# Splitting values that land by transposing transfers without priority, and leaving more work between the transfers out and back

## The chip, the cores and the metric

The kernel runs on one core of a Trainium2 chip. The metric is the device time of one execution in microseconds (us). The kernel before was run three times: 1028.9, 1032.0 and 1032.71 us, a median of 1032.0 us. TensorE (PE) multiplies matrices into PSUM banks; VectorE (DVE) and ScalarE (ACT) do elementwise work; GpSimd (POOL) does a few powers; SyncE (SP) issues nearly all transfers between the chip's main memory and the on-chip memory, and ACT issues a few.

## The reference

A sequence of 512 tokens of width 1024, with 16 learned meta tokens put in front, goes through two layers, and a final norm drops the meta tokens. Layer 0 is gated linear attention with 4 heads (keys of 256, values of 512); layer 1 is differential softmax attention with 8 heads (values of 256). Both have a wide input projection, a SiLU gate and an output projection:

```python
h = concat([meta, x])                          # 528 tokens
for i in range(2):
    hn = rmsnorm(h, g_norm[i])
    y = gla_branch(hn, ...) if i == 0 else diff_branch(hn, ...)
    h = h + y
return rmsnorm(h[:, 16:], g_final)

# gla_branch: q, k, v, z, g = split(hn @ w_in); decay = cumulative log-sigmoid of g
#   o = causal(q k^T with decay) v, per head;  y = silu(z) * head_rms(o) * gnorm;  y @ w_out
# diff_branch: q, k, v, z = split(hn @ w_in); p0, p1 = softmax(q k^T + bias) of two halves
#   o = (p0 - lam * p1) v, per head;  y = silu(z) * head_rms(o) * gnorm;  y @ w_out
```

All data are 32-bit floats. Every operand of a precise matmul is split into a high and a low part, and three products of the parts are summed.

## The kernel before

**Layout.** Activations stand with features on the 128 partitions and the 528 tokens along the row. A projection therefore gives q, k, v and z in this layout, too. The attention needs the values with tokens on the partitions, so v must be transposed, and then split into high and low parts for the matmuls that read it (the pair `s.v`, and `s.vm` for the 16 tokens left over of a multiple of 128).

**How v is turned.** In the heads 1 to 3 of layer 0, in two halves each, and once in each of the heads 1 to 6 of layer 1, this goes by way of main memory (`turn_by_dma`, L521): 12 times in all. It has four steps:

- `leave` (L530): ACT copies one of two blocks of v into 16-bit planes (L532) and issues the transfer out, to the buffer `vd` (L533). It runs once for each of the two blocks.
- `turn` (L538): SP issues transposing transfers back into the same place (L541; tile `keep` in layer 0, one each; `planes` in layer 1, two each) and one more, of the ends, into the single buffer `lands` (L543).
- `done` (L821 in layer 0, L1457 in layer 1): the landed values are split, ACT writing the high part (L262) and DVE the low part (L263), each about a microsecond of 128 x 1024 elements; and the ends are split by `split3`, two operations on ACT (L355, L356) and one on DVE (L360).
- The attention of that head reads the result: in layer 0 from `gla_blocks` on (L1129, first at L1141), in layer 1 in the step `values` of `diff_steps` (L1578).

Head 0 of layer 0, and the first and last heads of layer 1, turn v with TensorE instead and are not touched.

**Fill.** The `Weaver` W (L74) holds a queue of generators that emit projection matmuls a few at a time and state a cost in microseconds for each. The attention code calls `W.fill(us)` between its own steps so that TensorE always has something to do. `W.follow((a, f), (b, g))` calls f when a us of such fill have been emitted, and g when b us more have. `W.land()` (L1239, L1703), before a head's attention, calls whatever is left at once. A projection is emitted by `Unit` (L384): seven products of 12 matmuls each, with the first product of the next unit drawn ahead of the last two of its own.

**Order.** TensorE's instructions run in the order in which the program emits them (L212). For ACT, DVE and SP the framework makes an order: it goes through the program with its own reckoning of durations and gives each engine, when free, the operation of the best rank among those that it reckons ready. The rank is the place in the program; `@urgent` (L251) improves it by 100 places. The order is fixed at build time, so on the chip an engine waits at an operation whose input is late, with all that stands behind it.

**Other lines that the text names.** Weight loads are L271 and L278 (tile `raw`); weights are split at L262 and L263 (`wh`/`wl`, `a11h`/`a11l`, `a12`, `a22`); sums of weight blocks are L318 (`sum`, `raw`). `u` (L400) is a copy of a product on ACT, `t` L425 and L427 are the sums that finish a projection on DVE. L899 adds the output projection into `hT`, and TensorE's next product into the same bank (L891) waits for it. `on` (L1583, L1586) normalizes a block of attention rows in layer 1, and TensorE transposes it at L1592. `aT` and `am` are the split attention weights, `k` the split keys.

Of the kernel before, what the change touches and what calls it, by code (L numbers as in the profile page):

```python
# [150 lines left out]
class Weights:  # L151
# [44 lines left out]
    def done(self, p):  # L196
        self.room[p.kind] += 1
        self.pump()
# [8 lines left out]
def trunk(ctx, tc, x, meta, g_norm, gla_w_in, gla_w_gate_up, gla_b_gate, gla_gnorm, gla_w_out,  # L207
# [21 lines left out]
    def T(p, shape, dt, tag, **kw):  # L229
        uid[0] += 1  # L230
        return p.tile(shape, dt, tag=tag, name=f"{tag}_{uid[0]}", **kw)
# [27 lines left out]
    def split(hi, lo, src, scale=None):  # L259

        if scale is None:
            act.activation(hi, src, AF.Copy)  # L262
            dve.tensor_tensor(lo, src, hi.bitcast(F32), op=ALU.subtract)  # L263
        else:
            act.activation(hi, src, AF.Copy, scale=scale)
            dve.scalar_tensor_tensor(lo, src, scale, hi.bitcast(F32), op0=ALU.mult, op1=ALU.subtract)
# [27 lines left out]
    W = Weaver()  # L294
# [14 lines left out]
    def want_unit(w, c0):  # L309
        def single(tag, b):  # L310
            def fn(raw):
                t = [T(wp, [P, 512], F32R, tag + part, bufs=1) for part in "hl"]
                split(*t, raw[:, b, :])
                return t
            return Part(tag, fn)

        def add(o, a, b):
            dve.tensor_tensor(o, a, b, op=ALU.add)  # L318

        def sums(raw):  # L320
            t = T(wp, [P, 2, 512], F32, "sum", bufs=1)
            add(t[:, 1, :], raw[:, 2, :], raw[:, 3, :])
            add(t[:, 0, :], t[:, 1, :], raw[:, 0, :])
            add(raw[:, 2, :], raw[:, 2, :], raw[:, 0, :])
            return t

        def outer(raw):
            add(raw[:, 1, :], raw[:, 1, :], su.t[:, 0, :])
            ws.room["sum"] += 1
            return block_pair(raw[:, 1:3, :])  # L330

        a11, a12, a22 = single("a11", 0), single("a12", 1), single("a22", 3)
        su = Part("sum", sums)
        s21 = Part("pair", lambda raw: block_pair(su.t))
        s43 = Part("pair", outer)
        ws.want((w, c0), [a11, su, s21, a12, s43, a22])
        return a11, a12, a22, s21, s43
# [12 lines left out]
    def split3(dst, src, lo, scale=None):  # L350


        kw = {} if scale is None else {"scale": scale}
        hi = dst[:32].bitcast(F32)
        act.activation(dst[:32], src, AF.Copy, **kw)  # L355
        act.activation(dst[96 - lo:128 - lo], src, AF.Copy, **kw)  # L356
        if scale is None:
            dve.tensor_tensor(dst[lo:lo + 32], src, hi, op=ALU.subtract)
        else:
            dve.scalar_tensor_tensor(dst[lo:lo + 32], src, scale, hi, op0=ALU.mult, op1=ALU.subtract)  # L360
# [152 lines left out]
    def tmp():  # L513
        return T(tp, [P, L], F32, "t")


    def words(t):

        return t.bitcast(U16)

    def turn_by_dma(planes, groups, ends, done):  # L521

        n = planes.shape[2]
        vd = T(dp, [2, P, 2, n], U16, "vd", bufs=3)
        rows = vd.rearrange("m p h c -> (m p h) c")
        raw = planes.rearrange("p m c -> p (m c)")[:, :2 * NR].rearrange("p (b c) -> p b c", c=2 * P)
        left, lands = [0, 1], []

        @urgent
        def leave(m, src):  # L530
            pl = words(planes[:, m, :]).rearrange("p (h c) -> p h c", h=2)
            act.activation(pl, words(src).rearrange("p (c h) -> p h c", h=2), AF.Copy)  # L532
            act.dma_start(vd[m], pl)  # L533
            left.remove(m)
            if not left:
                W.follow((6.0, turn), (9.0, lambda: done(raw, lands[0][:32, 0, :])))

        def turn():  # L538
            for blocks, c0 in groups:
                o = words(raw[:, blocks, :])  # L540
                sp.dma_start(o, rows[:, c0:c0 + P * o.shape[1]], transpose=True)  # L541
            lands.append(T(mp, [P, 1, 2 * P], F32, "lands"))
            sp.dma_start(words(lands[0]), rows[:, ends:ends + P], transpose=True)  # L543

        return leave
# [237 lines left out]
    def to_tokens(vt, blocks, short_cols):  # L783


        pt, pm = ps_tile(), ps_tile()[:32, :P]
        for b, (t0, n) in enumerate(blocks[1:]):
            pe.transpose(pt[:, b * P:(b + 1) * P], vt[:, t0:t0 + n], ident)
        pe.transpose(pm, short_cols, ident)
        return pt, pm  # L790

    def plain_unit(u, evac):

        (a11, a22), (a12, a21) = [ws.use(h) for h in u]
        for i, (wa, wb) in enumerate(((a11, a12), (a21, a22))):
            banks = pb_pair()
            for j, (w, xs) in enumerate(((wa, (X["b11"], b12)), (wb, (X["b21"], X["b22"])))):
                for n, (k, p, q) in enumerate(PASSES):
                    for bank, x in zip(banks, xs):
                        pe.matmul(bank[:, :HT], w[p][:, k * P:(k + 1) * P], x[q][:, k, :],  # L800
                                  start=j == n == 0, stop=j == 1 and n == len(PASSES) - 1)
                    if n % 3 == 2:
                        yield 0.66
            evac(i, banks)
        for h in u:
            ws.done(h)

    def q_gla_v(hd, s):
        us = [want_unit(g_w_in, 2048 + 512 * hd + c) for c in (0, 256)] if hd else v_first

        def turned_back(m, vt):
            def post():
                pt, pm = to_tokens(vt, BLK, vt[:, :32])
                cs = slice(m * P, (m + 1) * P)
                split(s.v[0][:, :, cs], s.v[1][:, :, cs], pt.rearrange("p (b c) -> p b c", b=4))
                split3(s.vm[:, cs], pm, 32, short[:, NM:NM + 1])
            W.defer(2.4, post)

        def turner(h):
            @urgent  # L820
            def done(pt, pm):  # L821
                cs = slice(256 * h, 256 * h + 256)
                split(s.v[0][:, :, cs], s.v[1][:, :, cs], pt)
                split3(s.vm[:, cs], pm, 32, short[:, NM:NM + 1])
            return turn_by_dma(b_all[:, 2 * h:2 * h + 2, :], [(slice(0, 4), NM)], 0, done)

        gens = []
        for h, u in enumerate(us):
            vts = []

            def dst(h=h, vts=vts):
                if h == 0:
                    s.vm = T(gp, [M3, 512], F32R, "vm0")
                    s.v = [T(gp, [P, 4, 512], F32R, f"v{i}") for i in range(2)]
                vts.extend([tmp(), tmp()])
                return vts

            if hd:
                gens.append(W.add(Unit(u, X, 1.0, dst, lambda i, vts=vts, leave=turner(h): leave(i, vts[i]))))
            else:  # L840
                def evac(i, banks, h=h, vts=vts, dst=dst):
                    if i == 0:
                        dst()
                    for n, bank in enumerate(banks):
                        act.activation(vts[i][:, n * HT:(n + 1) * HT], bank[:, :HT], AF.Copy)
                    turned_back(2 * h + i, vts[i])

                gens.append(W.add(plain_unit(u, evac)))
        return gens[0]
# [593 lines left out]
    def turned_back2(s, m, vt, first=False):  # L1443
        if not first:

            urgent(dve.tensor_copy)(vt[:, HT:HT + 8], vt[:, 2 * HT:2 * HT + 8])

        @urgent
        def post():
            end = L if first else 272  # L1450
            pt, pm = to_tokens(vt, RBLK if first else HBLK, vt[:, end - 32:end])
            cs = slice(m * P, (m + 1) * P)
            split3(s.vm[:, cs], pm, 32, short[:, NM + 1:NM + 2])
            split(s.v[0][:, :, cs], s.v[1][:, :, cs], pt.rearrange("p (b c) -> p b c", b=4))

        @urgent
        def done(pt, pm):  # L1457
            split3(s.vm, pm, 32, short[:, NM + 1:NM + 2])
            split(s.v[0], s.v[1], pt)

        if first or s is heads[-1]:
            W.defer(2.2 if first else 1.4, post)
        else:
            if m:
                s.leave = turn_by_dma(T(ep, [P, 2, 536], F32, "planes", bufs=1),
                                      [(slice(3, 1, -1), 0), (slice(1, None, -1), 272)], 240, done)
            s.leave(m, vt[:, :536])
# [346 lines left out]
```

## Time and profile before

| what | value |
|---|---|
| median of three runs | 1032.0 us |
| the profiled execution | 1031.73 us |
| its span, first to last instruction | 1029.9 us |
| mean granted TensorE clock | 0.983 |
| busy, share of the span: PE, DVE, ACT, POOL | 95%, 76%, 60%, 5% |
| transfers out to `vd` on ACT, of 264 or 268 KB | 24 |
| transposing transfers on SP (L541 and L543) | 18 and 12 |

A row of the profile names the engine, the line of the kernel, the operation, the tile written and the tiles read, and their sizes. Waits are put down to what came last by the profile. The granted clock is the share of full speed that TensorE was given in a stretch. Idle time of an engine costs nothing by itself; it counts where TensorE waits for that engine.

### The profile page before, as it was taken

Reading aid. Unit: us, or ns where it says so; the run is one execution under the profiler, and the core shown is the slowest. Engines: PE = TensorE matmul, PEld = TensorE weight load, DVE = VectorE, ACT = ScalarE, POOL = GpSimd, SP = SyncE. Lnnn points to the kernel's source line nnn. Section 1 sums busy time; section 2 is a strip of 40 time slices with the busy share of each in tenths; the row PEclk is TensorE's granted clock in tenths of the full one; section 3 lists DMA queues with packets and bytes.
Section 4 is the critical chain, followed back from the end, with each engine's and each line's share of the span. In section 5 each row is a group of like instructions: output and inputs, shape, how many; then the busy total and the mean of one; then the engine's idle time right before and its main releaser. Section 6 shows DMA issues by size and latency. Waiting matters only on the chain. (4 is left out here: it accounts for less than half of the span.)

```text
span 1029.9 us, 18079 instructions
## 1 busy us (share of the span) xinstructions
PE 983.0 (95%) x7023; PEld 922.1 (90%) x7023; DVE 778.1 (76%) x1562; ACT 613.3 (60%) x1292; POOL 48.2 (5%) x68
## 2 busy tenths in 40 slices
PE   8999999899999998999999998998989999999997
PEld 7999999899989997999999797897978989978996
DVE  7888886687767886556996985877856868667785
ACT  6775756366626666536766674475654666645574
POOL 1000000000000100000001010000000000100001
PEclk8999999999999999999999999999999999999999
DMA  7222226331443354222323424234242333523212
GB/s 194 74 70 65 78 84 169 77 94 42 140 119 83 82 114 113 74 83 82 93 83 101 121 74 126 65 103 118 82 140 80 91 94 83 139 82 93 82 63 81
DMA packets 156296, 98.63 MB, mean 96 GB/s; under 512 B 38429, under 2 KB 142141, under 8 KB 156208
## 3 DMA queue, kind: packets, MB, share of 16 engines
q1 hardware_dynamic: 152752, 90.92, 32.8%
q10 hardware_dynamic: 3456, 6.54, 1.8%
q8 instruction: 55, 0.90, 0.4%
q14 instruction: 33, 0.27, 0.1%
HBM read 83.64 MB, written 8.66 MB: 90 GB/s over the span
## 5 line engine op out<-in xcount | busy, mean ns | idle before, releaser
L263 DVE TENSOR_TENSOR wl<-raw,wh 128x1024 fp32r<-128x1024 f32 x99 | 120.9, 1223 | 29.1 <-ACT wh L262 20.4
L262 ACT ACTIVATE wh<-raw 128x1024 fp32r<-128x1024 f32 x99 | 103.9, 1052 | 44.7 <-PE by L891 18.5
L379 PE MATMUL bv<-x,wh 128*128 128x264 f32 (+1 forms) x656 | 97.5, 287 | 3.2 <-DVE t L427 3.2
L379 PE MATMUL bx<-x,wh 128*128 128x264 f32 (+1 forms) x640 | 96.4, 288 | 4.2 <-ACT u L400 4.1
L379 PEld LDWEIGHTS bx<-x,wh 128*128 128x128 f32 x640 | 85.4, 190 | 5.8 <-ACT u L400 5.0
L379 PEld LDWEIGHTS bv<-x,wh 128*128 128x128 f32 x656 | 86.6, 189 | 3.9 <-DVE t L427 3.4
L369 PE MATMUL bx<-x,wh 128*128 128x512 f32 (+1 forms) x256 | 64.5, 395 | 2.6 <-ACT ps L1582 1.6
L263 DVE TENSOR_TENSOR wl<-sum,wh 128x1024 fp32r<-128x1024 f32 x41 | 50.1, 1222 | 21.0 <-ACT wh L262 19.6
L400 ACT ACTIVATE u<-bx 128x264 f32<-128x264 f32 (+1 forms) x120 | 45.4, 379 | 31.8 <-PE bx L379 28.5
L262 ACT ACTIVATE wh<-sum 128x1024 fp32r<-128x1024 f32 x41 | 43.2, 1054 | 25.3 <-PE by L891 8.6
L1549 ACT ACTIVATE p<-p,st 128x528 f32<-128x528 f32 (+3 forms) x64 | 36.4, 569 | 36.5 <-DVE st L1547 36.2
L369 PEld LDWEIGHTS bx<-x,wh 128*128 128x128 f32 x256 | 46.0, 195 | 11.6 <-ACT ps L1582 2.1
L379 PE MATMUL bv<-x,wl 128*128 128x264 f32 (+1 forms) x328 | 55.6, 287 | 0.0
L379 PE MATMUL bx<-x,wl 128*128 128x264 f32 (+1 forms) x320 | 53.6, 285 | 0.0
L1585 POOL TENSOR_TENSOR st<-st,mhalf 128x1 f32<-128x1 f32 x32 | 28.1, 878 | 495.0 <-ACT on L1583 420.1
L262 ACT ACTIVATE a11h<-raw 128x512 fp32r<-128x512 f32 x41 | 25.7, 626 | 37.3 <-DMA raw<-in_diff_w_in_dram 19.3
L379 PE MATMUL by<-x,a12h 128*128 128x264 f32 (+1 forms) x320 | 46.6, 286 | 0.0
L379 PEld LDWEIGHTS bv<-x,wl 128*128 128x128 f32 x328 | 46.4, 190 | 0.0
L379 PE MATMUL bx<-x,a11h 128*128 128x264 f32 (+1 forms) x320 | 46.2, 285 | 0.0
L379 PEld LDWEIGHTS bx<-x,wl 128*128 128x128 f32 x320 | 45.1, 189 | 0.6 <-DVE wl L263 0.5
L379 PEld LDWEIGHTS bx<-x,a11h 128*128 128x128 f32 x320 | 42.3, 189 | 0.8
L379 PEld LDWEIGHTS by<-x,a12h 128*128 128x128 f32 x320 | 41.7, 188 | 0.4 <-DVE t L425 0.2
(474 smaller groups left out, 2651.8 us busy)
## 6 DMA issues: line engine op xcount, KB each, us to landing
raw<-in_gla_w_in_dram SPq DMA_DIRECT2D x48, 512.0 KB, 5.3
raw<-in_diff_w_in_dram SPq DMA_DIRECT2D x42, 512.0 KB, 5.4
raw<-in_diff_w_in_dram SPq DMA_DIRECT2D x11, 1024.0 KB, 5.7
raw<-in_gla_w_out_dram SPq DMA_DIRECT2D x8, 1024.0 KB, 5.3
raw<-in_diff_w_out_dram SPq DMA_DIRECT2D x8, 1024.0 KB
vd<-planes ACTq DMA_DIRECT2D x12, 268.0 KB, 3.0
vd<-keep ACTq DMA_DIRECT2D x12, 264.0 KB, 2.2
T<-bdr SPq DMA_DIRECT2D x8, 264.0 KB, 3.6
```

The costliest lines, as they stand in the source:

```text
L262: act.activation(hi, src, AF.Copy)
L263: dve.tensor_tensor(lo, src, hi.bitcast(F32), op=ALU.subtract)
L369: pe.matmul(bank, a[:, k, :], b[k] if n0 is None else b[k][:, n0 + i * nn:n0 + (i + 1) * nn], start=n == 0 and ks[0] == 0, stop=n == len(t ...
L379: pe.matmul(bank[:, :x[q].shape[2]], w[p][:, k * P:(k + 1) * P], x[q][:, k, :], start=first and i == 0, stop=i == len(PASSES) - 1, skip_gr ...
L400: act.activation(t, self.bx[:, :self.n], AF.Copy, scale=self.sc)
L1549: act.activation(p[:, :nk], p[:, :nk], AF.Exp, scale=-1.0, bias=st[:, m:m + 1], accum_out=st[:, 2 + m:3 + m])
L1585: pool.tensor_tensor(ms, ms, mhalf[:, :1], op=ALU.pow)
```

## The change

The delays of `W.follow` in `turn_by_dma` go from 6.0 and 9.0 to 9.0 and 10.0 us of fill: `turn` is emitted 3 us of fill later, and `done` 4 us later in all. Both `done` functions lose `@urgent`, so that the five operations of each rank by their place in the program. Nothing else differs: the same instructions on the same engines, with the same operands.

```diff
@@ turn_by_dma, leave
             if not left:
-                W.follow((6.0, turn), (9.0, lambda: done(raw, lands[0][:32, 0, :])))
+                W.follow((9.0, turn), (10.0, lambda: done(raw, lands[0][:32, 0, :])))
@@ q_gla_v, turner
         def turner(h):
-            @urgent
             def done(pt, pm):
                 cs = slice(256 * h, 256 * h + 256)
                 split(s.v[0][:, :, cs], s.v[1][:, :, cs], pt)
@@ turned_back2
-        @urgent
         def done(pt, pm):
             split3(s.vm, pm, 32, short[:, NM + 1:NM + 2])
             split(s.v[0], s.v[1], pt)
```

## The prediction

> **What bounds the kernel now.** I read the page first: its busy shares, then its slices.
>
> ```profile
> span 1029.9 us, 18079 instructions
> PE 983.0 (95%) x7023; PEld 922.1 (90%) x7023; DVE 778.1 (76%) x1562; ACT 613.3 (60%) x1292; POOL 48.2 (5%) x68
> ```
>
> PE is busy for 95% of the span, so time comes back only where PE stands idle or runs at a low clock. Everything the change touches runs on ACT, DVE and SP, and counts only as far as it makes PE wait. I then read the waits of ACT and SP (engine, line, what it waited for: total us, times, longest), because the landed values are split on ACT and fetched by SP.
>
> ```profile
> ACT v L262 <- DMA planes<-vd: 25.3, 6, 6.8
> ACT v L262 <- DMA keep<-vd: 13.5, 6, 3.8
> SPq L541 <- DMA vd<-planes: 29.5, 6, 6.6
> SPq L541 <- DMA vd<-keep: 12.4, 5, 6.8
> ```
>
> All 12 splits are reached too early: ACT stands for 25.3 + 13.5 = 38.8 us before the values are there. SP likewise stands at the transposing transfer (L541), waiting for the transfer out. What this costs PE I took from PE's waits in the two stretches that hold the 12 places, 150 to 410 us (first layer) and 550 to 910 us (second).
>
> ```profile
> PE bv L891 <- DVE hT L899: 4.6, 2, 3.7
> PE bv L379 <- DVE t L427: 3.2, 1, 3.2
> PE bx L379 <- ACT u L400: 1.8, 1, 1.8
> PE by L891 <- DVE hT L899: 1.1, 1, 1.1
> PE bx L891 <- DVE t L425: 0.8, 1, 0.8
> ...
> PE ps L1592 <- ACT on L1586: 11.6, 6, 4.2
> PE ps L348 <- DVE aT L263: 1.7, 2, 0.9
> PE bx L369 <- ACT ps L1582: 1.6, 1, 1.6
> PE ps L348 <- ACT aT L262: 1.3, 2, 0.7
> PE bx L369 <- ACT wh L262: 1.0, 1, 1.0
> ```
>
> The first five are 11.5 us, the last five 17.2 us, together 28.7 us of PE idle, each piece within some 10 us of one of the 12 splits. It costs more than the idle. The table of windows (length, busy us of PE, PEld, DVE, ACT and POOL with counts, granted clock, DMA share, GB/s) has seven stretches at half clock, each just behind one of these places:
>
> ```profile
> 189.83:193.23 3.40, 3.40 (x17) 3.40 (x17) 1.30 (x3) 0.00 (x0) 0.00 (x0) 0.50 1.04 278
> 299.05:302.46 3.41, 3.41 (x18) 3.41 (x17) 1.51 (x3) 0.00 (x0) 0.00 (x0) 0.50 1.01 279
> ...
> sum 23.83, PE 23.33 PEld 21.37 DVE 14.82 ACT 11.83 POOL 0.55; mean PE 3.33 PEld 3.05 DVE 2.12 ACT 1.69 POOL 0.08
> ```
>
> Seven stretches, 23.8 us at half clock: half of it, 11.9 us or 1.7 us each, is lost. What lies around the 12 splits is thus worth at most 28.7 + 11.9 = 40.6 us.
>
> **The change part by part.** No instruction is added or removed, and TensorE's order, written out by hand, holds none of the moved ones. Moved in the program's order are 18 transposing transfers of values, 12 of ends (L543), and 60 compute instructions.
>
> *Is the place of a split the place where the program emits it?* The last of the 12 (start, duration, engine, line, operation):
>
> ```profile
> 885.24 1.08 ACT L532 ACTIVATE planes<-t 128x1072 uint16<-128x1072 uint16 x1
> 891.35 0.27 ACT L356 ACTIVATE am<-ps 32x128 fp32r<-32x128 f32 x1
> 896.25 1.06 ACT L262 ACTIVATE v<-planes 128x1024 fp32r<-128x1024 f32 x1 [4.63 <-DMA planes<-vd]
> 899.28 0.74 ACT L262 ACTIVATE k<-t 128x512 fp32r<-128x512 f32 x2 [0.17 <-DVE t L425]
> ```
>
> The program emits this split 6 + 9 = 15 us of TensorE fill after the last leaving copy (885.24). In ACT's order it stands right behind 891.35, 6.4 us after the copy, and ahead of the split of k, which the code emits about 8 us of fill after the copy (a unit is seven products of 1.32 us in the code's own measure, and k's first has run by then). So the planner has put it where it believed the values landed, not where it was emitted. Emission and priority are ranks: they decide only among operations that are ready together. I therefore cost the longer delays (6 to 9, 9 to 10) and the lost priority as lower ranks, and the places at which ACT stands at a landing at 0 for most of the 12. Bounds: the whole 40.6 us as a gain if all go; as a loss, the late transfers below.
>
> *The transposing transfers, three us of fill later.* SP waits at L541 for the transfer out (11 waits above), so the landing, not the emission, sets the issue: 0. If weight loads passed ahead, that is the slower rival.
>
> *Where a tie now goes the other way.* The second split of the first such head, on DVE and ACT:
>
> ```profile
> 183.83 0.47 DVE L360 SCALAR_TENSOR_TENSOR vm<-lands,short,vm 32x256 fp32r<-32x256 f32 x1 [2.47 <-ACT vm L355]
> 184.33 0.69 DVE L263 TENSOR_TENSOR a11l<-raw,a11h 128x512 fp32r<-128x512 f32 x1
> 188.48 0.43 DVE L899 TENSOR_TENSOR hT<-hT,bv 128x264 f32<-128x264 f32 x1
> 188.96 0.39 PE L891 MATMUL bv<-y,wh 128*128 128x264 f32 x1 [3.68 <-DVE hT L899]
> ```
>
> DVE stood 2.47 us for the small split of the ends (L360), with weight splits, sums and the addition that PE needed queued behind it. Without priority those go first. Part of the 2.47 us is then spent waiting for the second half of the weight load, which ACT also waited for here, so I take 1.9 of it (ends 0 and 2.47 + 0.47 = 2.9), and the half-clock stretch at 189.83 falls away: -1.9 - 1.7 = -3.6 us.
>
> The second split of the next head, on DVE:
>
> ```profile
> 293.84 1.23 DVE L263 TENSOR_TENSOR v<-keep,v 128x1024 fp32r<-128x1024 f32 x1 [0.66 <-ACT v L262]
> 295.08 0.47 DVE L360 SCALAR_TENSOR_TENSOR vm<-lands,short,vm 32x256 fp32r<-32x256 f32 x1
> 295.57 0.69 DVE L318 TENSOR_TENSOR raw<-raw 128x512 f32<-128x512 f32 x1
> 296.18 0.42 DVE L899 TENSOR_TENSOR hT<-hT,bv 128x264 f32<-128x264 f32 x1
> 296.66 0.39 PE L891 MATMUL bv<-y,wh 128*128 128x264 f32 x1 [0.95 <-DVE hT L899]
> 298.13 0.39 PE L891 MATMUL by<-y,wh 128*128 128x264 f32 x1 [1.09 <-DVE hT L899]
> ```
>
> The sum (L318) was ready and can now go into the 0.66 us in which DVE stood, and the 0.47 us of L360 falls back: 0.66 + 0.47, about -1.1 us of the 0.95 + 1.09 (ends 0 and 2.04). The stretch at 299.05 then goes as well, because 1.81 us of idle at 390 us brought no half clock: -1.1 - 1.7 = -2.8 us.
>
> At the third head ACT had this order:
>
> ```profile
> 390.47 0.51 ACT L356 ACTIVATE vm<-lands,short 32x256 fp32r<-32x256 f32 x1
> 391.00 0.63 ACT L262 ACTIVATE a11h<-raw 128x512 fp32r<-128x512 f32 x1
> 391.91 0.38 ACT L400 ACTIVATE u<-bx 128x264 f32<-128x264 f32 x1
> ```
>
> PE waited 1.8 us for u; with L356 behind it 0.51 us comes back (ends 0 and 0.51): -0.5. In the second layer nothing of a rank between the old and the new stood ready where ACT waited (k, hT and aT behind the split carry priority anyway): 0, with the 17.2 us left as they are.
>
> *What a late split could cost.* The last first-layer pair has the least slack:
>
> ```profile
> 407.56 0.47 DVE L360 SCALAR_TENSOR_TENSOR vm<-lands,short,vm 32x256 fp32r<-32x256 f32 x1
> ...
> 417.23 0.40 PE L1141 MATMUL ps<-vm,am 96*16 96x512 f32 x1
> ```
>
> It ends at 408.03; that head's first row block comes at 417.2, so 9.2 us cover it. In the second layer the values are those of the next head, so most of a head lies between. Cost 0 while the split slips by less than 9 us; past that, one for one.
>
> **Sum.** Against the profiled execution's 1031.73 us (span 1029.9 and 1.83 around it; 0.3 below the median, 1032.0): 1031.73 - 3.6 - 2.8 - 0.5 = 1024.8 us. The ends of the three are 0 and -2.9 - 1.7 - 2.0 - 1.7 - 0.5 = -8.8, so 1023 to 1032.
>
> [...]
>
> **The rivals.**
>
> *Nothing moves.* The ranks fall, but the planner finds the same order because nothing else is ready: 1031.7, within 0.5%. For it: the split's place at readiness, shown above. Against it: the operations standing right behind L360 in the two first-layer places.
>
> *The stalls go.* The splits slip behind other work by the mean wait of 38.8 / 12 = 3.2 us; half of the 40.6 us comes back: 1011.4. Against it: ACT is 60% busy, so there is seldom enough ready work to fill 3.2 us.
>
> *Slower: the transfers back go later and the splits do not.* With the later rank a weight load that is ready at the same moment goes ahead of L541 on SP and shares the DMA engines with it. ACT keeps its place and stands longer. PE loses 28.7 / 38.8 = 0.74 us per us of ACT's wait, so the 12 transfers would have to land 5.2 / (12 x 0.74) = 0.6 us later on average to pass 0.5%. For it: weight loads do follow directly, as behind the first of the second layer:
>
> ```profile
> 563.32 1.25 SPq L543 DMA_TRANSPOSE lands<-vd  x1
> 564.67 8.70 SPq L278 DMA_DIRECT2D raw<-in_diff_w_in_dram  x4
> ```
>
> If each lands later by the 1.25 us that one more transfer takes on SP in the first row, this is 12 x 0.74 x 1.25 = +11.1, 1042.8. Against it: in most places the loads wait for DVE to free their buffer. [...]
>
> **How the numbers follow.** Ties flip, 1024.8 (own range 1020 to 1030): 0.42, of which 0.30 beyond 0.5% (5.2 us, about what a measurement of this kernel can tell from no change) and 0.12 within. Nothing moves: 0.20, within. Stalls go: 0.14, faster. Transfers later: 0.24, of which 0.20 slower and 0.04 within. Faster 0.44, same 0.36, slower 0.20. The range, 1014 to 1042, leaves out about half of the stalls-go case (0.07) and of the slower one (0.10).
>
> **What would show it.** ACT's waits on planes and keep stay at 30 to 40 us in 12 waits. Near 184 us a11l runs before L360 and DVE's 2.47 us is gone; near 295 us L318 runs before the split; the half-clock stretches fall from seven to five, and those at 408 and in the second layer stay. The prediction is wrong if those 38.8 us fall by half (stalls go), if they grow (transfers later), or if the first-layer rows stay in their order.

## The result, and the profile after

The changed kernel took 1022.65 us, the median of five runs (1020.26 to 1023.65), beside 1029.3 us for the kernel before on the same chip (1028.9 to 1032.71, five runs). The medians lie 6.65 us apart, 0.6%. The ratio that goes with the interval, from all runs and not from the medians, is 0.9921 (0.8% faster) with a 95% interval of 0.9899 to 0.9943, that is 5.9 to 10.4 us. The forecast was 1024.8 us, 6.9 us below the execution profiled before.

The line numbers of the kernel after are one lower from L821 on and two lower from L1457 on: L891 and L899 have become L890 and L898, L1141 is L1140, and L1592 and L1586 are L1590 and L1584.

The page of the kernel after, its span and busy shares:

```profile
span 1021.2 us, 18077 instructions
PE 979.4 (96%) x7023; PEld 918.1 (90%) x7023; DVE 778.2 (76%) x1562; ACT 612.9 (60%) x1292; POOL 48.2 (5%) x68
```

The span is 8.7 us shorter than before (1029.9). PE was busy for 3.6 us less with the same 7,023 matmuls: up to the last of them, the stretches at a granted clock of 0.50 add up to 30.7 us before and 23.9 us after, and half of the difference is 3.4 us. To see in which part the time went, I use the matmuls of the leftover tokens (L1141, L1140 after), of which there is one per head of the first layer. In the summary of that line the columns after the count are the duration in ns (minimum, median, maximum) and the start of the first and of the last. First the kernel before, then the kernel after:

```profile
L1141 PE MATMUL ps<-vm,am x4: 399/399/399, 110.7 to 417.2; 96*16 96x512 f32 x4
```

```profile
L1140 PE MATMUL ps<-vm,am x4: 399/399/399, 108.3 to 408.0; 96*16 96x512 f32 x4
```

The first of the four stands ahead of every place that the change touches, and the last behind the last place of the first layer. The six first-layer places lie between them: 306.5 us before, 299.7 us after, so 6.8 us came back there. (Half of it is idle and half is clock: PE's waits from 150 to 410 us, without those in the attention blocks that stayed as they were, fell from 11.5 to 8.1 us, and of three stretches at half clock, each 3.41 us at 0.50 and so 1.7 us, one is left.) From the last one to the end of the span it was 612.7 us and is now 613.2. The remaining 2.4 us were gained before 108 us, where the programs don't differ. There the execution profiled before had a stretch at half clock that the one profiled after did not have (a clock of 1.00 from 17 to 24 us):

```profile
19.20:26.00 6.80, 6.28 (x27) 5.76 (x27) 6.76 (x11) 3.47 (x7) 0.00 (x0) 0.50 0.43 50
```

That is a difference between two executions and not the change. What the change itself did in the profile, 6.8 - 0.5 = 6.3 us, lies within the interval of the times.

**ACT's waits** in the kernel after (total us, times, longest):

```profile
ACT v L262 <- DMA planes<-vd: 25.0, 6, 6.5
ACT v L262 <- DMA keep<-vd: 14.9, 6, 3.7
```

All twelve splits still come too early, by 39.9 us in all (38.8 before). What changed is the order of the small operations behind them. **The second split of the first such head**, in the timeline of the kernel after (rows of DVE and PE, picked out):

```profile
179.08 0.69 DVE L263 TENSOR_TENSOR a11l<-raw,a11h 128x512 fp32r<-128x512 f32 x1
...
182.34 0.42 DVE L898 TENSOR_TENSOR hT<-hT,bv 128x264 f32<-128x264 f32 x1
182.82 0.39 PE L890 MATMUL bv<-y,wh 128*128 128x264 f32 x1
183.82 0.42 DVE L898 TENSOR_TENSOR hT<-hT,by 128x264 f32<-128x264 f32 x1
184.27 0.48 DVE L360 SCALAR_TENSOR_TENSOR vm<-lands,short,vm 32x256 fp32r<-32x256 f32 x1
184.29 0.39 PE L890 MATMUL by<-y,wh 128*128 128x264 f32 x1 [1.09 <-DVE hT L898]
```

L360 was ahead of a11l, with 2.47 us of DVE standing before it; now it is behind both additions into `hT`. PE's 3.68 us of idle have become 1.09, on the next bank: a weight split of 1.22 us now runs between the two additions, at 182.68. **The same place of the next head**, picked out likewise:

```profile
286.14 0.69 DVE L318 TENSOR_TENSOR raw<-raw 128x512 f32<-128x512 f32 x1
...
287.34 1.22 DVE L263 TENSOR_TENSOR v<-keep,v 128x1024 fp32r<-128x1024 f32 x1
288.48 0.42 DVE L898 TENSOR_TENSOR hT<-hT,bv 128x264 f32<-128x264 f32 x1
288.90 1.23 DVE L263 TENSOR_TENSOR wl<-raw,wh 128x1024 fp32r<-128x1024 f32 x1
288.95 0.39 PE L890 MATMUL bv<-y,wh 128*128 128x264 f32 x1 [0.23 <-DVE hT L898]
290.05 0.42 DVE L898 TENSOR_TENSOR hT<-hT,by 128x264 f32<-128x264 f32 x1
290.50 0.48 DVE L360 SCALAR_TENSOR_TENSOR vm<-lands,short,vm 32x256 fp32r<-32x256 f32 x1
290.52 0.39 PE L890 MATMUL by<-y,wh 128*128 128x264 f32 x1 [1.18 <-DVE hT L898]
```

The sum (L318) runs ahead of the split and L360 behind the additions; 0.95 + 1.09 us of idle have become 0.23 + 1.18. PE's waits in the kernel after, from 150 to 410 us, show what is left in the first layer:

```profile
PE bx L379 <- ACT u L400: 4.6, 2, 2.9
PE by L890 <- DVE hT L898: 2.3, 2, 1.2
```

The 4.6 us are the third head. The wait for `u` that was 1.8 us is 1.6, and ACT's order there is the one it was before:

```profile
381.58 0.51 ACT L356 ACTIVATE vm<-lands,short 32x256 fp32r<-32x256 f32 x1
382.11 0.63 ACT L262 ACTIVATE a11h<-raw 128x512 fp32r<-128x512 f32 x1
383.02 0.38 ACT L400 ACTIVATE u<-bx 128x264 f32<-128x264 f32 x1
```

At that head's second split PE had waited 3.2 us for the sum L427, which ran on DVE behind the split of the values (at 407.10, the split at 405.96). Now the sum runs ahead of the split (393.97 and 397.40), and PE waits 2.9 us for the next `u` (399.38), which stands behind the split on ACT. The table of windows of the kernel after (length, busy us of PE, PEld, DVE, ACT and POOL with counts, granted clock, DMA share, GB/s) has these:

```profile
182.50:189.00 6.50, 5.28 (x41) 4.89 (x40) 5.44 (x11) 1.13 (x2) 0.00 (x0) 1.00 0.61 161
288.00:296.00 8.00, 6.59 (x53) 6.18 (x52) 6.90 (x12) 1.93 (x2) 0.00 (x0) 1.00 0.48 132
400.60:404.00 3.40, 3.40 (x18) 3.40 (x17) 2.36 (x4) 2.55 (x5) 0.00 (x0) 0.50 0.74 251
561.00:564.40 3.40, 3.40 (x10) 2.63 (x9) 2.52 (x6) 3.40 (x11) 0.00 (x0) 0.50 0.07 18
704.40:707.80 3.40, 3.40 (x9) 2.65 (x8) 3.40 (x7) 0.95 (x3) 0.00 (x0) 0.51 0.71 198
```

Behind the first two places the clock is now full. But there are again seven stretches at half clock: the last of the first layer (now at 400.6 us), the four of the second layer (now at 622.4, 759.0, 840.9 and 895.5 us), and two in the second layer that are new, at 561.0 and 704.4 us.

### The profile page after: what moved, and what is told of

Same layout as the page of the kernel before. It is cut to its first block, busy times and chain, and to the rows that moved or that the text cites. A ratio compares the mean times of both kernels' runs of the same rounds, so it can differ in the third digit from the quotient of the medians.

```text
span 1021.2 us, 18077 instructions
## 1 busy us (share of the span) xinstructions
PE 979.4 (96%) x7023; PEld 918.1 (90%) x7023; DVE 778.2 (76%) x1562; ACT 612.9 (60%) x1292; POOL 48.2 (5%) x68
## 5 line engine op out<-in xcount | busy, mean ns | idle before, releaser
L379 PEld LDWEIGHTS bx<-x,wh 128*128 128x128 f32 x640 | 84.8, 189 | 7.4 <-ACT u L400 6.5
L369 PE MATMUL bx<-x,wh 128*128 128x512 f32 (+1 forms) x256 | 69.1, 416 | 0.0
L369 PEld LDWEIGHTS bx<-x,wh 128*128 128x128 f32 x256 | 49.4, 208 | 9.9 <-ACT wh L262 0.3
```

The lines of the kernel that those rows point to most:

```text
L369: pe.matmul(bank, a[:, k, :], b[k] if n0 is None else b[k][:, n0 + i * nn:n0 + (i + 1) * nn], start=n == 0 and ks[0] == 0, stop=n == len(t ...
L379: pe.matmul(bank[:, :x[q].shape[2]], w[p][:, k * P:(k + 1) * P], x[q][:, k, :], start=first and i == 0, stop=i == len(PASSES) - 1, skip_gr ...
```

## The experiments

My theory was that the gain is a matter of rank in the first layer alone, at the two places above, and that the splits did not move. The rivals were that the longer delays do it, that both layers share it, and that ACT's early waiting can be had back only by really moving the splits. For the kernels before and after and the eight edits, the time in the profile from the first to the last row of L1141 (the first layer's places) and from there to the end of the span (the second layer), worked out as above, and the ratio to the kernel before on the same chip:

| kernel | first-layer places, us | rest, us | median, us | ratio, 95% interval |
|---|---|---|---|---|
| before | 306.5 | 612.7 | 1029.3 | |
| after | 299.7 | 613.2 | 1022.65 | 0.9921 (0.9899 to 0.9943) |
| first layer without priority | 298.9 | 612.9 | 1024.87 | 0.9910 (0.9878 to 0.9941) |
| second layer without priority | 306.4 | 614.8 | 1031.74 | 0.9967 (0.9949 to 0.9985) |
| longer delays only | 307.3 | 613.7 | 1034.77 | 1.0002 (0.9980 to 1.0024) |
| ends without priority, first layer | 300.7 | 610.9 | 1027.22 | 0.9944 (0.9926 to 0.9962) |
| placed, delays 6 and 6 | 291.3 | 593.3 | 998.02 | 0.9637 (0.9609 to 0.9665) |
| placed, delays 9 and 10 | 295.2 | 597.1 | 1003.63 | 0.9714 (0.9694 to 0.9735) |
| placed in the second layer only | 307.2 | 594.7 | 1016.37 | 0.9839 (0.9819 to 0.9858) |
| placed, with priority | 294.6 | 596.0 | 1002.68 | 0.9704 (0.9681 to 0.9726) |

The kernel before had a median of 1033.93 us beside the first three of these edits and the placed kernel with 6 and 6, and 1032.79 us beside the other four; so the ratios are what is to be compared, and differences in us below are to the median of the same chip. The two columns from the profile are of one execution each, and a stretch at half clock more or less (3.41 us at 0.50) moves them by up to 1.7 us.

**First layer without priority**

```diff
         def turner(h):
-            @urgent
             def done(pt, pm):
```

> Only the first layer's `done` loses its priority; the delays stay 6.0 and 9.0, and the second layer stays as it was. Theory (ties of rank in the first layer): nearly the whole gain is here, 5 to 8 us below the kernel before, with the half-clock stretches near 190 and 299 us gone and ACT's waits on planes and keep still 30 to 40 us. Rival (the longer delays make the gain): within 1 us of the kernel before. Rival (the gain is spread over both layers): 2 to 4 us below.

Measured: 0.9910, 9.1 us between the medians, with an interval that overlaps that of the whole change. The first layer's places took 298.9 us, as after the change (299.7), and the rest 612.9. No stretch at half clock stands near 190 or 299 us. The delays are thus not needed for the gain, and the first layer holds it. The size is above the 5 to 8 us that I expected, by no more than the interval allows (6 to 13 us).

**Second layer without priority**

```diff
-        @urgent
         def done(pt, pm):
             split3(s.vm, pm, 32, short[:, NM + 1:NM + 2])
```

> Only the second layer's `done` loses its priority; delays and first layer as before. Theory (ties of rank in the first layer): within 1 us of the kernel before, since the small splits of the ends that move behind a weight split and k had nothing waiting behind them that TensorE needed. Rival (gain spread over both layers): 2 to 4 us below. Rival (the lost priority in the second layer costs, and the first layer pays for it): 1 to 2 us above.

Measured: 0.9967, 2.2 us between the medians. By its interval (1.6 to 5.3 us faster) this is not the zero of my theory, and it lies in the range of the rival that both layers share the gain. It is less than the 0.5% that I took as what a measurement of this kernel can tell from no change. The profile does not settle it: PE's waits between 535 and 912 us sum up to 17.4 us, against 18.3 in the kernel before, but the rest took 614.8 us against 612.7, in an execution with six windows at half clock in the second layer where the one before had four. Unclear; a gain of a few microseconds in the second layer is not excluded.

**Longer delays only**

```diff
-                W.follow((6.0, turn), (9.0, lambda: done(raw, lands[0][:32, 0, :])))
+                W.follow((9.0, turn), (10.0, lambda: done(raw, lands[0][:32, 0, :])))
```

> Only the delays change, 6.0 and 9.0 to 9.0 and 10.0; both `done` functions keep their priority. Theory (priority decides the ties): a later rank of some 30 places does not undo a priority of 100, so the split of the ends (L360) stays ahead of a11l near 184 us and ahead of L318 near 295 us; DVE's wait of 2.47 us and both half-clock stretches stay; 0 to 1.5 us below the kernel before. Rival (the longer delays make the gain): 5 to 8 us below. Rival (the transfers back go later): above the kernel before, ACT's waits on planes and keep grow past 45 us.

Measured: 1.0002. The timeline near the second split of the first such head:

```profile
185.74 0.47 DVE L360 SCALAR_TENSOR_TENSOR vm<-lands,short,vm 32x256 fp32r<-32x256 f32 x1 [2.05 <-ACT vm L355]
186.25 0.69 DVE L263 TENSOR_TENSOR a11l<-raw,a11h 128x512 fp32r<-128x512 f32 x1
...
190.40 0.42 DVE L899 TENSOR_TENSOR hT<-hT,bv 128x264 f32<-128x264 f32 x1
190.88 0.59 PE L891 MATMUL bv<-y,wh 128*128 128x264 f32 x1 [3.80 <-DVE hT L899]
```

L360 keeps its place ahead of a11l, DVE stands for 2.05 us and PE for 3.80, and the stretch at half clock behind it is there, at 190.4 us. Near 298 us L360 (298.21) stays ahead of L318 (298.70), too. But the stretch behind that place, which I expected to stay, is not there; the last section has the idle in the windows around it. ACT's waits on `planes` and `keep` were 26.4 and 14.5 us, 40.9 together, and 41.0 in the first edit, which has the old delays: the transfers back did not land later in any way that shows. So the longer delays did nothing by themselves that the interval of 0.2% would show, neither the gain nor the loss that the slower rival feared.

**Ends without priority, first layer**

```diff
         def turner(h):
-            @urgent
             def done(pt, pm):
                 cs = slice(256 * h, 256 * h + 256)
-                split(s.v[0][:, :, cs], s.v[1][:, :, cs], pt)
+                urgent(split)(s.v[0][:, :, cs], s.v[1][:, :, cs], pt)
                 split3(s.vm[:, cs], pm, 32, short[:, NM:NM + 1])
```

> In the first layer only the three operations on the ends (L355, L356, L360) lose their priority; the split of the values keeps it; delays and second layer as before. Theory (what matters is that L360 no longer stands ahead of a11l, L318 and the additions into hT): most of the gain of the first-layer edit, 5 to 8 us below the kernel before; near 295 us L318 stays behind the split of the values, so of the 1.1 us of TensorE's idle there only about half comes back. Rival (the split's own priority makes the gain): within 2 us of the kernel before.

Measured: 0.9944, 5.6 us between the medians, and 300.7 us for the first layer's places against 298.9 with the split's priority gone too. The difference, 1.8 us, is about what one stretch at half clock costs (1.7 us): there is one at 387.4 us, behind a wait of 2.05 us for `u` that was 1.32 us in the other execution, which has no such stretch. PE's waits from 150 us to the last of these places sum up to nearly the same, 9.6 us here and 9.0 there, and the two ratios' intervals overlap. So most of the first layer's gain is the three small operations on the ends; that the priority of the large split adds anything is not shown.

**Placed, delays 6 and 6.** The remaining rival was that the stalls themselves go. To test it the splits had to be put where the program emits them. This kernel is the changed one, with each `done` tied on ACT behind the last ACT instruction emitted before it:

```diff
-                W.follow((9.0, turn), (10.0, lambda: done(raw, lands[0][:32, 0, :])))
+                W.follow((6.0, turn), (6.0, lambda: behind(tc, done, raw, lands[0][:32, 0, :])))
...
+def behind(tc, fn, *a):
+    last = next(i for i in reversed(tc.nc.cur_bb.bb.instructions)
+                if i.engine == mybir.EngineType.Activation)
+    with tc.issue_after(last):
+        fn(*a)
```

`issue_after` lets the framework place what is emitted inside it only behind the given instruction on that engine. The profile has the same number of operations as before on TensorE, DVE and ACT.

> The changed kernel with delays 6.0 and 6.0, and the five operations of `done` tied on ACT behind the last ACT instruction that the program has emitted by then, so that each split really stands 12 us of fill behind the last leaving copy, and not where the planner believes its values to have landed. Tests the rival that the stalls go. If ACT's early waiting is what TensorE's idle around the 12 places comes from: ACT's waits on planes and keep fall from 39 to under 10 us, TensorE's idle at L1592, L348 and L369 in the second layer falls from 17 to under 9 us, and the time is 12 to 20 us below the kernel before. If that idle comes from other causes (DVE's load, the chain of an attention block): ACT's waits fall just as much, but the time is no more than 8 us below, as with the changed kernel.

Measured: 0.9637, 35.9 us between the medians, and well beyond what even the theory expected. The span, and ACT's only remaining wait on the landed values (it also stood 1.3 us for ends):

```profile
span 996.0 us, 18078 instructions
```

```profile
ACT v L262 <- DMA keep<-vd: 2.1, 1, 2.1
```

The last of the twelve, in its timeline, without a wait:

```profile
862.08 0.27 ACT L356 ACTIVATE am<-ps 32x128 fp32r<-32x128 f32 x1
...
864.89 0.74 ACT L262 ACTIVATE k<-t 128x512 fp32r<-128x512 f32 x2 [0.32 <-DVE t L425]
...
874.88 0.51 ACT L356 ACTIVATE vm<-lands,short 32x256 fp32r<-32x256 f32 x1
875.41 1.06 ACT L262 ACTIVATE v<-planes 128x1024 fp32r<-128x1024 f32 x1
```

Before, this split stood right behind that `am` (L356), with 4.63 us of waiting; now the splits of `k`, two weight splits and steps of the attention run in between. PE's waits in the same two parts of the kernel, as far as they lie near the twelve places. From 150 to 410 us:

```profile
PE by L891 <- DVE hT L899: 1.1, 1, 1.1
PE bv L891 <- DVE hT L899: 1.0, 1, 1.0
```

and in the second layer:

```profile
PE ps L1592 <- ACT on L1586: 4.2, 2, 3.4
PE bx L379 <- ACT u L400: 1.1, 1, 1.1
PE ps L348 <- DVE q L266: 0.5, 1, 0.5
PE ps L348 <- DVE yt L1595: 0.2, 1, 0.2
```

The wait of 1.1 us for `u` in the second layer stood before, too, and is not among the 28.7 us of idle near the twelve places. Of these 7.0 are left, and of the seven stretches at half clock two remain, at 82.6 us (ahead of the twelve places) and at 560.5 us. This kernel also lost the priority; with the same tie and the priority kept (the last experiment) some 11 of the 28.7 us are left. So ACT's 39 us of early waiting was the cause of most of that idle.

**Placed in the second layer only**, in the kernel before, with its priority:

```diff
-                W.follow((6.0, turn), (9.0, lambda: done(raw, lands[0][:32, 0, :])))
+                W.follow((6.0, turn), (9.0, lambda: done(raw, lands[0][:32, 0, :]))) if n < 536 else W.follow((6.0, turn), (6.0, lambda: behind(tc, done, raw, lands[0][:32, 0, :])))
```

> The kernel before, with priority and first layer unchanged; in the second layer alone the splits are placed 12 us of fill behind the last leaving copy (delays 6.0 and 6.0). Theory (TensorE's idle near each place is ACT's early waiting, place by place): the second layer gives back what it gave with both layers placed, 17 to 21 us below the kernel before, and the first layer's gaps near 184, 295, 390 and 404 us stay. Rival (the gain needs the lost priority): under 8 us below.

Measured: 0.9839, 16.4 us between the medians. The second layer took 594.7 us, as with both layers placed (593.3), and the first layer's places 307.2, as before. The gain sits place by place, and the second layer's half of it needs no lost priority.

**Placed, delays 9 and 10**: the same tie, with the change's own delays.

```diff
-                W.follow((9.0, turn), (10.0, lambda: done(raw, lands[0][:32, 0, :])))
+                W.follow((9.0, turn), (10.0, lambda: behind(tc, done, raw, lands[0][:32, 0, :])))
```

> The changed kernel with its own delays, 9.0 and 10.0, and the splits really placed where the program emits them. In the second layer that is at the start of the next head's attention, where the program calls whatever is left; the values are read some 27 us later, so it costs nothing there. In the first layer the second split of the third head moves some 10 us back to about 403 us, while the profile with 6.0 and 6.0 has its first use at 402.7 us. Theory (the place of the split is what counts, as long as it is ahead of its use): 25 to 35 us below the kernel before, that is 1 to 8 us worse than with 6.0 and 6.0, and the loss stands as a TensorE wait for v or vm near 403 us. Rival (the gain of 6.0 and 6.0 came from shorter delays): no more than 12 us below.

Measured: 0.9714, 29.2 us between the medians. PE's new wait stands where it was expected:

```profile
404.53 0.59 PE L1141 MATMUL ps<-vm,am 96*16 96x512 f32 x1 [4.67 <-DVE vm L360]
```

This is the price of a split that comes too late: here the split of the third head's second half ran at 401.6 us and its ends at 403.9, and the first block that reads them stood for 4.67 us. The rest, where I expected no cost, took 597.1 us against 593.3. Some 2 us of that belong to the same wait: the profile shows half clock from 401.96 to 408.79 us, and 4.26 us of this lie behind the start of the row above. What makes up the remaining 1.7 us stays open.

**Placed, with priority**: the kernel before with the tie and delays of 6.0 and 6.0.

```diff
-                W.follow((6.0, turn), (9.0, lambda: done(raw, lands[0][:32, 0, :])))
+                W.follow((6.0, turn), (6.0, lambda: behind(tc, done, raw, lands[0][:32, 0, :])))
```

> The kernel before with both `done` functions at their priority, and the splits of both layers placed 12 us of fill behind the last leaving copy (delays 6.0 and 6.0). Theory (once a split stands behind its landing, priority has nothing to hold up): within 4 us of the kernel with 6.0 and 6.0 without priority, that is 32 to 38 us below the kernel before. Rival (priority is half of the gain): 12 to 25 us below.

Measured: 0.9704, 30.1 us between the medians, a little under the 32 to 38 expected: the theory that priority then has nothing to hold up does not hold. The order near 290 us tells what priority still costs. DVE in this kernel:

```profile
289.88 0.47 DVE L360 SCALAR_TENSOR_TENSOR vm<-lands,short,vm 32x256 fp32r<-32x256 f32 x1
...
291.60 1.22 DVE L263 TENSOR_TENSOR wl<-raw,wh 128x1024 fp32r<-128x1024 f32 x1
292.73 0.42 DVE L899 TENSOR_TENSOR hT<-hT,bv 128x264 f32<-128x264 f32 x1
```

L360, two sums and a weight split stand ahead of the addition into `hT`, and PE waited 2.92 us for it, against 0.99 with the priority gone. So both edits of the kind matter, the place by some 30 us and the priority, on top of it, by some 6.

## Why the prediction was right

*What moves, and what does not.* Right. ACT's 38.8 us of waits stayed (39.9), because the framework places a split where it reckons that its values have landed, and the emission only ranks it. The placed kernels show this from the other side: with the same emission and a tie, the waits go.

*The second split of the first head, -3.6.* Right in its parts: the idle went from 3.68 to 1.09, which is 2.6 us where I had taken 1.9 (and 2.9 as the end), and the stretch at half clock behind it went (1.7). I had guessed that part of the stall would be spent on the second half of the weight load. In fact DVE stood only 0.17 us for a load there, and L360 fell behind both additions.

*The next head, -2.8.* The order came as described, L318 ahead of the split and L360 back. But of the 1.1 us only 0.6 came back (0.95 + 1.09 to 0.23 + 1.18), because a weight split (`wl`, 1.23 us) stands between the two additions into `hT`, after as before, and the second idle piece is its doing and not that of L360. The stretch at 299 us went, but its 1.7 us are in part luck. It was there in three of the four profiles with the old order (before, the second layer without priority, and placed in the second layer only). In the fourth, with the longer delays only, an edge between windows cut through the same two waits (0.82 and 1.27 us on its two sides), and the clock stayed full. My reason was an accident, too: the 1.81 us of idle at 390 us, behind which the clock stayed full, lay across such an edge at 391.21 (0.68 and 1.13 us on its two sides); in the other three of these four profiles 1.8 to 1.9 us at that place lay in one window, and half clock followed each time.

*The third head, -0.5.* Right in size (0.2 + 0.3) and wrong in the mechanism, so this is luck. I had L356 fall behind `u`; it did not, as the three rows of ACT above show, and the 0.2 us are not its doing. The 0.3 us came at a place that I had not foreseen: the 3.2 us wait for L427 turned into 2.9 us for `u`, since L427 now runs ahead of the split of the values. The stretch behind it stayed, as I said, but that also goes by how the wait falls: with the first layer's priority alone gone, PE stood there for 3.06 us, in two windows, and no half clock followed.

The three sum to -7.1 by these readings, against -6.9 forecast, and the first layer measured -6.8: a wait of 0.8 us for L425 elsewhere grew to 1.0.

*The second layer, 0, with its stretches at half clock unchanged.* The sum held (+0.5), but not the rows: I said that the seven stretches would fall to five, and there are seven again. The step that failed is the assumption that a stretch belongs to a gap and stays or goes with it. PE's waits in the second layer even fell, from 18.3 to 16.5 us, while two more windows ran at half clock; the two nearly cancel, so that the sum of 0 was luck as well. In these profiles half clock went with how a gap falls into the windows described in the last section. The bound of 40.6 us for both layers held: the placed kernel returned 34.6 of it (15.2 + 19.4 by the table), partly by the lost priority.

*The rivals.* "Nothing moves" fails on the rows. "Transfers back go later" fails on the run with the delays alone: 1.0002, and 40.9 us of waits on ACT, no more than the 41.0 with the old delays. "The stalls go" was given 0.14, for the wrong reason of the splits slipping by chance; it did not happen here. I also argued against it that ACT, 60% busy, seldom has enough ready work to fill 3.2 us. That argument was wrong: with the splits tied, ACT found work for nearly all of the time, and the case was worth 36 us (some 6 of them by the lost priority) and not 20.

On the clock, the prediction went by its own trace, in which 2.04 us of idle ahead of 299.05 us had half clock behind them and 1.81 us at 390 us had not. The ten profiles fit that, as the last section shows: each of the 38 windows with more than 1.9 of its 3.41 us idle was followed by one at half clock. The place of their grid of 3.413 us against the span's start differs by 0.9 us between the profiles before and after (stretches start at 189.82 and at 400.56 us).

## What to carry to other kernels

Where a framework orders an engine's work by its own reckoning, moving the emission of an operation or its priority changed only ties here; if the profile shows the engine standing at an operation whose input comes by transfer, tie the operation behind other work of that engine and measure how far back it may go before its reader waits. Take small operations that nobody needs soon off any priority: here the split of the ends (L360) held DVE for 2.47 us ahead of the addition that TensorE needed, and PE stood for 3.68 us; after the change it was 1.09. And take the bound on such a gain from TensorE's own idle around the places and the stretches at half clock behind them: here 40.6 us, of which tying the operations, together with the lost priority, returned 34.6.

## What the runs showed of the hardware

In these profiles the stretches at half clock do not start where a gap ends: before, PE's wait of 0.95 us ended at 296.66 and the one of 1.09 us at 298.13, and half clock began at 299.05. Within one execution their starts lie on one grid of 3.413 us: 160.4, 61.4, 82.0, 54.6, 81.9 and 54.6 us lie between the seven starts of the kernel after, which is 47, 18, 24, 16, 24 and 16 times 3.413 to within the 0.1 us to which I set the windows. I sorted the windows of that grid by TensorE's idle inside each. In the ten profiles (before, after and the eight edits), from 30 us to the end of the matmuls, there are 2,850 such windows. Each of the 38 with more than 1.9 us of idle was followed by one at half clock. Of those between 1.4 and 1.9 us, 9 were and 23 were not. Of those below 1.4 us only two were, and both stood at half clock themselves. The kernel before shows both sides; the first row is of the window ahead of the stretch at 299.05 (2.04 us idle), the second of one behind which the clock stayed full (1.77 us idle):

```profile
295.64:299.05 3.41, 1.37 (x9) 1.10 (x9) 3.41 (x7) 0.18 (x1) 0.00 (x0) 1.00 0.04 11
708.65:712.06 3.41, 1.64 (x6) 1.03 (x6) 3.34 (x7) 1.63 (x7) 1.22 (x1) 1.00 0.01 2
```

The run with the longer delays only has no stretch near 299 us: its two waits there leave 0.82 and 1.27 us of idle in two windows that follow each other, where the kernel before had 2.04 us in one. The kernel placed with priority has three windows of its grid at full clock around its wait of 2.92 us, with 1.50, 1.42 and 0.00 us of idle in them:

```profile
288.38:291.79 3.41, 1.91 (x16) 1.70 (x15) 3.11 (x5) 2.17 (x4) 0.00 (x0) 1.00 0.00 0
291.79:295.21 3.42, 2.00 (x14) 1.85 (x15) 3.42 (x7) 0.00 (x0) 0.00 (x0) 1.00 0.27 68
295.21:298.62 3.41, 3.41 (x30) 3.41 (x29) 2.38 (x5) 1.06 (x1) 0.00 (x0) 1.00 0.84 237
```

And this is how the kernel after came by its stretch at 704.4 us. Before, PE waited at that place for 0.95 us (`wh`, up to 708.6 us) and for 2.06 us (`on`, up to 712.35 us), in three windows. Now it waits once, 2.45 us for `on`, and all of that lies in one window, with 0.96 us of PE's work:

```profile
700.94:704.35 3.41, 0.96 (x6) 0.82 (x6) 3.38 (x8) 2.29 (x8) 0.57 (x1) 1.00 0.38 108
```

The 1.7 us that I booked for each stretch (3.41 us at 0.50) thus came behind 2.04 us of idle in one window of the kernel before and 2.45 us in one of the kernel after, and not behind 1.81 us that lay in two windows.
